# V and gate columns of all sixteen heads by Strassen, masks added by matmul, one projection unit per differential head

## The chip, the cores and the metric

The kernel runs on one core of a Trainium2 chip. The metric is device microseconds of one execution, the median of three runs. Five engines of the core appear in the profile: TensorE (PE, its weight loads PEld), VectorE (DVE), ScalarE (ACT), GpSimd (POOL) and SyncE (SP). DMAs are issued from the queues of SP, ACT and POOL and share 16 DMA engines.

## The reference, cut to what matters

One layer, 1024 tokens, width 2048. One projection feeds two groups of eight heads; each group has q, k, v and gate columns of width 1024.

```
hn = rmsnorm(x, norm_mix_g)                       # (1024, 2048)
proj = hn @ w_in                                  # (2048, 8192)
sb_q, sb_k, sb_v, sb_g, df_q, df_k, df_v, df_g = split(proj, -1)
# stick-breaking group: A[t,s] = beta_ts * prod_{s<j<t}(1-beta_tj), s < t
# differential group, partial rotary on 16 of 64 columns of each q and k half:
s  = q_c @ k_c.T * 64**-0.5,  c = 0, 1;   pr_c = softmax(where(mask, s, -inf))
df = (pr_0 - lam * pr_1) @ v;  df = rmsnorm(df, subln_g) * (1 - lambda_init)
mixed = concat([sb * silu(sb_g), df * silu(df_g)])
h = x + mixed @ w_out
h = h + sigmoid(rmsnorm(h, norm_ple_g) @ w_ple_gate) * (p @ w_ple_proj)
return rmsnorm(h, norm_final_g)
```

## The kernel before

All operands are float32. A product of two of them is made of three matmuls: each operand is split into a high part (a cast to fp32r, on ScalarE) and a low part (the difference, on VectorE), and high x high, high x low and low x high are accumulated in PSUM (L240 to L242, L634 to L636, L1750 to L1752). Activations lie transposed, features on partitions and 512 tokens (a *half*) as columns, with the token order reversed; the half with index 1 holds the first 512 tokens and is computed first.

The program has four stages.

1. *First stage* (to about 331 us). The V and gate columns of the eight stick-breaking heads, for both halves, by one level of Strassen's scheme: `Seven` (L585) runs seven products per unit in place of eight. A unit is one head; there are two phases, one for each half of the 2048 features, and a product is 12 matmuls of 128x512 (`product`, L629). Weights are loaded (`wload`, L672), combined by VectorE (`sources`, L683), split (`whigh`, `wlow`, L711 and L728), and results leave by `vput` (L839) to `vghalf_d` (phase 0), are read back as `hr` in phase 1, added, and written to `vg_d`. Sums of x for the next phase (`visit`, L977) and sums of squares of x (`squares`, L1031) are made alongside.
2. *Heads* (L1335 on): for each half, first the differential heads 8 to 15, then the stick-breaking heads 0 to 7. `unit` (L226) is 96 matmuls over four weight pieces of 128x1024 and gives 256 columns of the projection. A stick-breaking head has one unit (q, k) and reads V and gate from `vg_d`. A differential head has two: one for q and k, one for V and gate. Weight pieces are loaded by SP and split in `wprep` (L149; ScalarE L162, VectorE L157). After q and k are evicted (`taken`), the rotary steps and the splitting of q and k follow on VectorE and ScalarE.
3. *Output projection* by `Seven`, then 4. *the gate, the embedding and the last norm*.

Order: TensorE, VectorE and ScalarE run in the order in which the code emits instructions. Inside a head, `Side` (L199) holds a list of steps with a due time, counted in steps of three matmuls; `unit` ticks it after each group of three, so attention of one head (`attention`, L289: scores, `weights`, `values`, `turn`, `mix`, `norm`) is spread between the projection matmuls of the next heads. Due times are written out as numbers. Scores get their causal mask from VectorE, which adds a 128x128 tile in PSUM (`masked`, L320 to L326); in the fourth row block the differential score is one matmul of 256 columns (`side_by_side`, L312), since k's tile holds high and low parts side by side.

Two lines say what the rest hangs on, the units of the projection stream and the due times of a differential head:

```
units = [(ap["w_in"][hd][i], half, hd) for half, order in ((1, ORDER1), (0, ORDER0)) for hd in order for i in range(1 if hd < H else 2)]
s0, s1, s2, t0 = [0, 2], [5, 8], [12, 15], 19
```

## Time and profile before

| what | value |
|---|---|
| time, median of 3 | 2430.82 us (2429.68 to 2435.75) |
| profiled execution, its own time | 2428.5 us |
| its span | 2426.7 us |
| granted TensorE clock | 0.994 |
| DMA moved | 492.92 MB, mean 203 GB/s |
| chain that ended last | PE 84%, DVE 6%, DMA 4%, ACT 3% |

How to read the lines that follow in the prediction. A group's row gives line, engine, operation, tiles as out<-in, shapes and count; behind the first bar the busy time and the mean duration of one in ns; behind the second the idle time of that engine just before, and what ended it. A wait's row gives waiter, releaser, total us, times, longest. A window's row gives its length, then busy us (and count) of PE, PEld, DVE, ACT and POOL, the granted clock, the DMA engines' busy share and GB/s. A timeline row gives start and duration in us. Matmul durations are latencies that overlap, so their pace has to be read from starts.

### The profile page before, as it was taken

How to read it: one execution, taken by the hardware profiler on the slowest of the kernel's cores; microseconds unless marked ns; L12 is line 12 of the kernel's file. 1: busy time of each engine (PE TensorE's matmuls, PEld its weight loads, DVE VectorE, ACT ScalarE, POOL GpSimd, SP SyncE). 2: the span in 40 equal slices, each digit the busy share in tenths (PEclk: the TensorE clock that was granted, in tenths of full speed). 3: DMA queues.
4: the chain of work that ended last, by engine and by line, in shares of the span. 5: the costliest groups of instructions: out<-in, count | busy, mean ns of one | idle time of the engine just before them, and what ended most of it. 6: DMA issues, size and time to landing. Idle time of an engine off the chain costs nothing.

```text
span 2426.7 us, 32432 instructions
## 1 busy us (share of the span) xinstructions
PE 2364.6 (97%) x11262; PEld 1966.1 (81%) x11262; DVE 1862.1 (77%) x3233; ACT 1194.5 (49%) x2138; POOL 243.7 (10%) x368
## 2 busy tenths in 40 slices
PE   9999999999999999999999999999999998999997
PEld 7777878888888887888888888887778886878876
DVE  7887867777877777788888866667787877577788
ACT  6243335555556445555556566445534434532453
POOL 1211100000000000000000001011121221001000
PEclk9999999999999999999999999999999999999999
DMA  7876755444456777444444465667788999898965
GB/s 234 303 253 232 239 180 156 152 156 131 135 150 223 245 252 241 122 114 112 111 125 117 112 188 171 203 200 233 196 220 217 263 266 296 273 321 280 320 206 178
DMA packets 221604, 492.92 MB, mean 203 GB/s; under 512 B 24768, under 2 KB 37056, under 8 KB 221440
## 3 DMA queue, kind: packets, MB, share of 16 engines
q1 hardware_dynamic: 158224, 345.86, 43.6%
q0 software_dynamic: 43920, 109.86, 18.4%
q10 hardware_dynamic: 19296, 35.14, 4.2%
q8 instruction: 88, 1.44, 0.2%
q14 instruction: 76, 0.62, 0.1%
HBM read 336.09 MB, written 163.05 MB: 206 GB/s over the span
## 4 chain that ended last, share of the span: by engine, by line
PE 84%; DVE 6%; DMA 4%; ACT 3%; issue 2%; SPq 0%; ACTq 0%; POOL 0%; DVEq 0%; POOLq 0%
PE acc L242 14%; PE acc L240 14%; PE acc L241 14%; PE pbc L634 4%; PE pbc L635 4%; PE pbc L636 4%; PE tp L415 2%; PE z L319 1%; PE z L318 1%; PE pb L1750 1%; PE pb L1751 1%; PE pb L1752 1%; PE av L462 1%; PE av L461 1%; PE av L460 1%
## 5 line engine op out<-in xcount | busy, mean ns | idle before, releaser
L240 PE MATMUL acc<-xh,whi 128*128 128x512 f32 x1152 | 465.8, 404 | 0.0
L242 PE MATMUL acc<-xh,wlo 128*128 128x512 f32 x1152 | 452.1, 392 | 4.1 <-DVE wlo L157 4.1
L241 PE MATMUL acc<-xl,whi 128*128 128x512 f32 x1152 | 451.6, 392 | 0.0
L162 ACT CAST whi<-wraw 128x1024 fp32r<-128x1024 f32 x192 | 201.6, 1050 | 121.5 <-PE acc L241 113.9
L242 PEld LDWEIGHTS acc<-xh,wlo 128*128 128x128 f32 x1152 | 217.1, 188 | 53.4 <-DVE wlo L157 5.4
L725 ACT CAST wpr<-T 128x512 fp32r<-128x512 f32 x144 | 87.5, 620 | 341.9 <-DVE T L690 260.6
L241 PEld LDWEIGHTS acc<-xl,whi 128*128 128x128 f32 x1152 | 218.1, 189 | 37.7
L240 PEld LDWEIGHTS acc<-xh,whi 128*128 128x128 f32 x1152 | 217.4, 189 | 38.0
L157 DVE TENSOR_TENSOR wlo<-wraw,whi 128x1024 fp32r<-128x1024 f32 x160 | 195.1, 1220 | 49.4 <-ACT whi L162 48.0
L434 ACT CAST awh<-tp 128x256 fp32r<-128x256 f32 (+1 forms) x160 | 80.7, 504 | 162.2 <-PE tp L415 160.7
L370 ACT ACTIVATE et<-z,mx 128x512 f32<-128x512 f32 (+7 forms) x128 | 94.7, 740 | 61.7 <-DVE mx L364 53.3
L725 ACT CAST wpr<-wraw 128x512 fp32r<-128x512 f32 x112 | 68.5, 614 | 108.6 <-DMA wraw<-tw_d 38.6
L439 DVE TENSOR_TENSOR awl<-tp,awh 128x256 fp32r<-128x256 f32 (+1 forms) x160 | 92.3, 577 | 37.0 <-ACT awh L434 36.7
L349 DVE TENSOR_TENSOR_SCAN st<-pt 128x511 f32<-128x511 f32 (+3 forms) x64 | 86.7, 1355 | 24.2 <-ACT pt L342 22.7
L739 DVE TENSOR_TENSOR wpr<-wraw,wpr 128x512 fp32r<-128x512 f32 x112 | 76.0, 684 | 35.3 <-ACT wpr L725 35.1
L739 DVE TENSOR_TENSOR wpr<-T,wpr 128x512 fp32r<-128x512 f32 x144 | 98.6, 685 | 3.7 <-ACT wpr L725 1.1
L364 DVE TENSOR_REDUCE mx<-z 128x1 f32<-128x512 f32 (+7 forms) x128 | 97.0, 758 | 4.4
L634 PE MATMUL pbc<-cS,wpr 128*128 128x512 f32 x208 | 81.2, 390 | 1.4 <-DVE u L1111 1.1
L635 PE MATMUL pbc<-cS,wpr 128*128 128x512 f32 x208 | 80.9, 389 | 0.0
L636 PE MATMUL pbc<-cS,wpr 128*128 128x512 f32 x208 | 80.9, 389 | 0.0
L326 DVE TENSOR_TENSOR z<-z,masks 128x128 f32<-128x128 f32 x144 | 42.2, 293 | 45.9 <-PE z L316 31.5
L342 ACT ACTIVATE pt<-z 128x512 f32<-128x512 f32 (+3 forms) x64 | 41.6, 650 | 71.8 <-DVE z L326 69.9
(548 smaller groups left out, 6203.6 us busy)
## 6 DMA issues: line engine op xcount, KB each, us to landing
wraw<-w_in SPq DMA_DIRECT2D x192, 512.0 KB, 3.7
wraw<-w_gate SPq DMA_DIRECT2D x92, 256.0 KB, 5.8
wraw<-w_out SPq DMA_DIRECT2D x72, 256.0 KB, 4.5
wlo_d<-wlo SPq DMA_DIRECT2D x32, 512.0 KB, 3.0
wlo<-wlo_d SPq DMA_DIRECT2D x32, 512.0 KB, 3.4
wraw<-w_vg SPq DMA_DIRECT2D x58, 256.0 KB, 3.5
comb_d<-sg POOLq DMA_DIRECT2D x48, 256.0 KB, 7.4
h_d<-hc POOLq DMA_DIRECT2D x48, 256.0 KB, 4.8
```

Of the source, the lines that this page charges most:

```text
L157: V.tensor_tensor(lo[:, o], raw[:, o], hi[:, o].bitcast(F32), op=ALU.subtract)
L162: side.later(1, lambda: A.copy(hi[:, o], raw[:, o]))
L240: T.matmul(acc[c], hi[:, k2, kh, c, :], xh, start=first, stop=False)
L241: T.matmul(acc[c], hi[:, k2, kh, c, :], xl, start=False, stop=False)
L242: T.matmul(acc[c], lo[:, k2, kh, c, :], xh, start=False, stop=last)
L364: V.reduce_max(mx, z[:, vw], axis=AX.X, negate=True)
L370: A.activation(et[:, vw], z[:, vw], AF.Exp, bias=mx[:, 0:1], accum_out=l)
L634: T.matmul(o, wh[:, w], xh, start=start and k == 0, stop=False, skip_group_check=True)
L635: T.matmul(o, wh[:, w], xl, start=False, stop=False, skip_group_check=True)
L636: T.matmul(o, wl[:, w], xh, start=False, stop=k == 3, skip_group_check=True)
L725: A.copy(t[:, 0], src)
L739: V.tensor_tensor(t[:, 1], src, t[:, 0].bitcast(F32), op=ALU.subtract)
```

## The change

- The first stage makes V and gate of all sixteen heads: `Seven` with 16 units. The first product pair of heads 8 to 15 in phase 0 runs ahead as plain products (`opening`). Phase 1 no longer reads phase 0's results back: `vput` accumulates into `vg_d` in DRAM. The sums of squares of x move to phase 0.
- In phase 1, `weight_pieces` loads 30 pieces of the differential heads' q and k weights, splits them and stores high and low parts in `whi_d` and `wlo_d`. In the first half these pieces, and in the later half all pieces, are read from there (stick-breaking heads 3 to 7 of the later half read the raw weights and the low part).
- A differential head has one unit. The rotary columns of q and k are gathered into one tile `rot` by SBUF to SBUF DMAs, turned once for both, and copied back; the high parts go to q, qz and k by DMA too. V and gate come from `vg_d`.
- Masks of the differential scores are added by a bf16 matmul, identity x mask, between the two score matmuls; in the first half both softmaxes' scores share one PSUM tile (`pairs`). The fourth row block uses two matmuls of 256 columns.
- In the later stages operands of the gate are loaded in another order and the gate's products run A11 three times before A12; the last unit's S1 product comes after S3. Due times of all steps are new numbers.

The core of the diff:

```diff
-            units = [(ap["w_in"][hd][i], half, hd) for half, order in ((1, ORDER1), (0, ORDER0)) for hd in order for i in range(1 if hd < H else 2)]
+            units = [(ap["w_in"][hd][i], half, hd) for half, order in ((1, ORDER1), (0, ORDER0)) for hd in order for i in range(1)]
...
+    def is_made(pc, half, hd):
+        return half == 0 or hd >= H and 4 * (hd - H) + pc < PIECES
...
+        if made:
+            nc.sync.dma_start(hi.bitcast(F32), whi_d[hd, pc].bitcast(F32))
+            lastw[0] = nc.sync.dma_start(lo.bitcast(F32), wlo_d[hd, pc].bitcast(F32))
+            return hi, lo
...
-                elif side_by_side:
-                    T.matmul(o, q[:, c, rs], k[:, c, 3 * P:], start=True, stop=True)
...
                     T.matmul(o, q[:, c, rs], k[:, c, c0:HALF], start=True, stop=False)
+                    if ki == 0:
+                        T.matmul(z[:, rs], identb, masks[:, 1, :], start=False, stop=False, skip_group_check=True)
                     T.matmul(o, qz[:, c, rs], KL[:, ki, c0:], start=False, stop=True)
...
+        def pairs(rb):
+            z = pz.tile([P, 2, HALF], F32, name="z", tag="z")
...
-        gv = Seven(lambda u, ph, k: ap["w_vg"][u, ph, k], H, flow(H))
+        gv = Seven(lambda u, ph, k: ap["w_vg"][u, ph, k], 2 * H, flow(2 * H))
...
         def vput(o, ph, hf, blk, u):
-            G.dma_start((vg_d if ph else vghalf_d)[hf, blk, u], o)
+            G.dma_start(vg_d[hf, blk, u], o, **(dict(accum_op=ALU.add) if ph else {}))
...
+        def weight_pieces(u):
...
+                    nc.sync.dma_start(lo.bitcast(F32), ap["w_in"][hd][0][pc].rearrange("p a b c d -> p (a b c d)"))
+                def fn(hd=hd, pc=pc, lo=lo, hi=hi):
+                    A.copy(hi, lo.bitcast(F32))
+                    V.tensor_tensor(lo, lo.bitcast(F32), hi.bitcast(F32), op=ALU.subtract)
+                    for d, t in ((whi_d, hi), (wlo_d, lo)):
+                        G.dma_start(d[hd, pc].rearrange("p a b c d -> p (a b c d)").bitcast(F32), t.bitcast(F32))
...
-                if ph:
-                    V.tensor_tensor(u2, u2, r[1, 1], op=ALU.add)
...
-                if ph:
-                    gv.xq.extend((gv.slot + 3, fn) for fn in squares(u))
+                if ph and 2 * u < PIECES:
+                    weight_pieces(u)
+                if ph == 0 and 0 < u < 9:
+                    gv.xq.extend((gv.slot + 3, fn) for fn in squares(u - 1))
...
-        NEXT = {"A11": [("A11", 0)], "A12": [("A12", 0)], "S1": [("A11", 4)]}
+        NEXT = {"A11": [("A11", 0)], "S3": [("A11", 4, 3)], "S1": [("A11", 7, 1), ("A12", 0)]}
...
+                        for b in range(2):
+                            m = 64 * c + 32 * b
+                            nc.sync.dma_start(fs["r"].bitcast(F32)[m:m + 32, :], f[64 * b:64 * b + 32, :])
...
+                    def high(c, fs=fs, qk=qk):
+                        h = fs["sr"[c]]
+                        A.copy(h, fs[c].bitcast(F32))
+                        for b, r in enumerate(rows):
+                            for t, o in ((qk[0], r), (qk["qz"], r)) if c == 0 else ((qk[1], rows[0]), (qk[1], rows[1])):
+                                nc.sync.dma_start(t[o, b, 0:HALF].bitcast(F32), h[r].bitcast(F32))
...
-                    vacc = two_accs()
-                    unit(X, acc=vacc)
...
-GAPS, GAPD = 4, 6
+SC = ((20.5, 21, 23.5, 25.5, 29.5, 31.5, 34.0, 37.0), (24.5, 27, 34, 41))
+ROPE = ((3.5, 4.0, 6.0, 10.0, 11.6, 12.5, 15.0), (6.5, 7, 9.5, 12.5, 12.6, 13.5, 14))
```

Where instructions stand now. TensorE, the first scores of the first differential head of the half computed first; `z` is the score tile, `kl` and `qz` the low parts, `acc` the projection of the next unit. Before:

```order
L318 MATMUL z<-k,q 128x512
L319 MATMUL z<-kl,qz 128x512
L240 MATMUL acc_3248<-cA11h,whi 128x512
L241 MATMUL acc_3248<-cA11l,whi 128x512
L242 MATMUL acc_3248<-cA11h,wlo 128x512
```

Now:

```order
L427 MATMUL z<-k,q 128x512
L429 LDWEIGHTS identb
L429 MATMUL z<-masks,identb 128x128
L430 MATMUL z<-kl,qz 128x512
L427 MATMUL z<-k,q 128x512
L429 LDWEIGHTS identb
L429 MATMUL z<-masks,identb 128x128
L430 MATMUL z<-kl,qz 128x512
```

Both softmaxes' scores of a row block follow each other without projection matmuls between, each with a mask matmul and its own weight load in the middle.

SP's queue over one differential head of the half computed first; `wraw` is a raw weight piece, `mixed_d` and `comb_d` take a head's result. Before:

```order
L169 DMA wraw<-w_in 128x1024 x5
L1493 DMA h_d<-xT 128x512 x2
L169 DMA wraw<-w_in 128x1024 x3
L270 DMA mixed_d<-sg 128x512
L278 DMA comb_d<-neg 128x512 x3
```

Now (`rot` holds the rotary columns, `qk` the evicted q or k, `sw` and `rot` later also the high parts):

```order
L1612 DMA rot<-qk 32x512 x2
L183 DMA whi<-whi_d 128x1024
L184 DMA wlo<-wlo_d 128x1024
L1513 DMA vf<-vg_d 128x512
L1612 DMA rot<-qk 32x512 x2
L1513 DMA gf<-vg_d 128x512
L183 DMA whi<-whi_d 128x1024
L184 DMA wlo<-wlo_d 128x1024
L1629 DMA qk<-rot 32x512 x4
L291 DMA mixed_d<-sg 128x512
L299 DMA comb_d<-neg 128x512 x3
L1636 DMA q<-sw 64x512
```

The small copies stand between the weight loads on one queue, and each waits for VectorE or ScalarE.

POOL's queue in phase 1 of the first stage; `hc` is a result of a product, `wpiece` a weight piece. Before:

```order
L840 DMA vghalf_d<-hc 128x512 x13
L840 DMA vg_d<-hc 128x512 x25
L1339 DMA cs<-rope 128x2x512
L840 DMA vg_d<-hc 128x512 x7
L1428 MEMSET qz 128x1024 x2
```

Now:

```order
L950 DMA vg_d<-hc 128x512 x3
L1210 DMA whi_d<-wpiece 128x1024
L1210 DMA wlo_d<-wpiece 128x1024
L1210 DMA whi_d<-wpiece 128x1024
L950 DMA vg_d<-hc 128x512
L1210 DMA wlo_d<-wpiece 128x1024
L950 DMA vg_d<-hc 128x512 x3
```

Four stores of weight pieces, 512 KB each, stand among the four accumulating stores of a unit.

More of the change, by code (lines that the diff above doesn't have):

```diff
@@ L355, in three @@
                     ws[rb] = bt
-                side.later(1, one)
-                side.later(3, two)
-                side.later(5.5, three)
+                side.later(SBL[half][0], one)
+                side.later(SBL[half][1], two)
+                side.later(SBL[half][2], three)
                 return
@@ L475, in summed @@
                         mixed(half, hd, sg)
-            side.later(2, summed)
+            side.later(2 if sb else LM[half][1], summed)
             if sb:
@@ L493, in low @@
                 sqs[pr] = sq, sqh, sql
[L495 to L496 removed]
+            side.later(LM[half][2], squared)
+            side.later(LM[half][3], low)
         def norm(pr):
@@ L554, in attention @@
             if not sb:
-                steps.append((t + gap * n + (7 if tight else NORM_LAT), partial(norm, pr)))
+                steps.append((t + gap * n + NORM_LAT[half][pr], partial(norm, pr)))
         return steps
@@ new lines, in _body @@
+        gv.xq.extend((0, fn) for fn in todo)
+        for u in range(H, 2 * H, 2):
+            pair = []
+            for nm in ("A11", "A12"):
+                for j in range(2):
+                    if nm == "A11":
+                        pair.append(pp.tile([P, HALF], F32, name="pa", tag="acc", bufs=2))
+                    prod(u + j, 0, nm, pair[j], nm == "A11")
+                    o = ftile()
+                    A.copy(o, pair[j])
+                    if nm == "A11":
+                        G.dma_start(vgpart_d[u + j], o)
+                    else:
+                        vput(o, 0, 1, 0, u + j)
@@ L1085, in _body @@
         prev = None
         for ph in range(2):
[L1087 to L1095 removed]
+            for u in range(2 * H):
+                last = ph == 1 and u == 2 * H - 1
+                s1 = ev.tile([P, HALF], F32, name="s1", tag="sq", bufs=2)
```

596 lines of the change are left out of this document (365 added, 231 removed).

## The prediction

> **What bounds the kernel now.** I read the page first, its engine row and the summary of the chain that ended last:
>
> ```profile
> PE 2364.6 (97%) x11262; PEld 1966.1 (81%) x11262; DVE 1862.1 (77%) x3233; ACT 1194.5 (49%) x2138; POOL 243.7 (10%) x368
> PE 84%; DVE 6%; DMA 4%; ACT 3%; issue 2%; SPq 0%; ACTq 0%; POOL 0%; DVEq 0%; POOLq 0%
> ```
>
> PE holds 84% of the chain, so a matmul taken away is worth its pace and a wait of PE is worth its length. Next, busy time by stage: the differential heads of the half computed first, with 512 keys (331:740), and of the later half, with 1024 keys (960:1430); then the stretches from the output projection on. Columns: length, busy us of PE, PEld, DVE, ACT, POOL, clock, DMA share, GB/s.
>
> ```profile
> 331.00:740.00 409.00, 405.78 (x1914) 337.91 (x1913) 312.92 (x659) 219.82 (x432) 19.10 (x31) 1.00 0.47 144
> 960.00:1430.00 470.00, 467.82 (x2343) 395.34 (x2342) 383.89 (x698) 271.34 (x465) 32.18 (x45) 1.00 0.43 119
> 1690.00:1800.00 110.00, 103.62 (x510) 84.25 (x509) 85.21 (x137) 58.82 (x110) 18.64 (x22) 1.00 0.82 214
> 1800.00:1900.00 100.00, 99.50 (x440) 82.03 (x439) 80.48 (x128) 38.32 (x67) 19.44 (x25) 1.00 0.87 227
> 1900.00:2024.00 124.00, 122.77 (x539) 100.55 (x538) 99.33 (x153) 48.35 (x86) 35.69 (x51) 1.00 0.98 274
> 2024.00:2100.00 76.00, 67.91 (x280) 53.92 (x279) 46.66 (x74) 38.63 (x67) 5.66 (x8) 0.96 0.86 270
> 2100.00:2200.00 100.00, 94.59 (x408) 77.11 (x408) 70.33 (x115) 39.67 (x73) 10.78 (x15) 0.98 0.96 310
> ```
>
> The head stages leave PE almost no idle time and use less than half of the DMA engines; idle time sits in later stretches, where the DMA share is 0.82 to 0.98. The view of waits names PE's longest ones:
>
> ```profile
> PE pbc L634 <- DVE hc L1138: 5.0, 2, 2.6
> PE acc L242 <- DVE wlo L157: 4.6, 3, 2.2
> PE pa L1751 <- DVE cgA12l L619: 4.5, 1, 4.5
> ...
> PE pbc L634 <- DVE hc L1081: 3.5, 2, 2.7
> ```
>
> A busy matmul time is no price, since matmuls overlap. The timeline of PE gives the pace, start to start (first column; between the first two rows lie eleven more matmuls of 128x512):
>
> ```profile
> 902.04 0.39 PE L240 MATMUL acc<-cA12h,whi 128*128 128x512 f32 x1
> ...
> 904.80 0.28 PE L314 MATMUL z<-k,q 128*128 128x256 f32 x1
> 904.91 0.28 PE L315 MATMUL z<-k,q 128*128 128x256 f32 x1
> 905.03 0.28 PE L316 MATMUL z<-k,q 128*128 128x256 f32 x1
> 905.15 0.40 PE L240 MATMUL acc<-cA12h,whi 128*128 128x512 f32 x1
> ```
> ```profile
> 1693.91 0.60 PE L415 MATMUL tp<-ident,bt 128*128 128x128 f32 x4
> 1694.27 0.48 PE L634 MATMUL pa<-cA11h,wfhi 128*128 128x512 f32 x1
> ```
>
> So 2.76/12 = 0.230 us at 512 columns, 0.35/3 = 0.117 at 256, 0.36/4 = 0.09 for a 128x128 transpose; at 384 I take 0.17, between the first two.
>
> **The change part by part.**
>
> *Projection.* Sixteen second units (8 differential heads, 2 halves) of 96 matmuls go: 1536. Eight more Strassen units come: 8 x 2 phases x 7 products x 12 = 1344. Net 192 x 0.230 = 44.2 us less.
>
> *Scores.* In 32 score tiles (fourth row block) one matmul of 256 columns becomes two: 32 x 0.117 = 3.7 us more.
>
> *Masks.* 128 bf16 matmuls of 128x128 are new. No row shows bf16. From below, a quarter of a 512 matmul, 0.058; from above a whole one, 0.23, should the change of type or the extra weight load break the overlap; work added to a full PE excludes a gain. I take the nearest row, the transpose: 128 x 0.09 = 11.5 us (7.4 to 29.4). The masks that VectorE loses ended none of PE's long waits.
>
> *VectorE and ScalarE in the heads.* The unit that goes was cover: such a head had 470/8 = 58.8 us of PE and 48.0 of VectorE in the later half. By my count of matmuls it now has 116 of 512, 4 of 384, 52 of 256 and 38 of 128 columns: 26.7 + 0.7 + 6.1 + 3.4 = 36.9 us (29.0 in the first half, by 100, 4, 28 and 22). VectorE loses, by these groups,
>
> ```profile
> L157 DVE TENSOR_TENSOR wlo<-wraw,whi 128x1024 fp32r<-128x1024 f32 x160 | 195.1, 1220 | 49.4 <-ACT whi L162 48.0
> ...
> L326 DVE TENSOR_TENSOR z<-z,masks 128x128 f32<-128x128 f32 x144 | 42.2, 293 | 45.9 <-PE z L316 31.5 <-PE z L319 13.8
> ...
> L1458 DVE STREAM_SHUFFLE sw<-qk 128x512 f32<-128x512 f32 x32 | 23.5, 734 | 0.0
> ...
> L1450 DVE TENSOR_TENSOR q<-qk,q 64x512 fp32r<-64x512 f32 x32 | 22.0, 686 | 0.9
> ...
> L1454 DVE TENSOR_TENSOR k<-qk,k 64x128 fp32r<-64x128 f32 x64 | 18.1, 283 | 0.4
> ```
>
> 8 x 1.22 (weights now come split from DRAM), 10 masks at 0.29, one shuffle and three rotary products (0.73 + 3 x 0.69), and of 4 x 0.69 + 4 x 0.28 for q and k all but 2 x 0.69: 9.8 + 2.9 + 2.8 + 2.5 = 18.0. So 30.0 of 36.9, a share of 0.81 where it was 0.82; 39.1 - 18.0 = 21.1 of 29.0 in the first. I cost this at nothing: the share that hid it before hides it still. If that cover fails, the second rival is the price.
>
> *Waits that go.* The three waits on wlo L157 (4.6) fall with the subtraction: the first pieces of a half are fetched made. The gate operands are loaded in another order and A12's are first used one product later, which aims at the wait on cgA12l (4.5). 9.1 us less; either may come back as a wait on a DMA (0 to 9.1). The waits on hc (8.5) are PSUM banks that VectorE reads late; the four adds per unit of phase 1 that filled its queue there go, but units double. I leave them (plus or minus 8.5).
>
> *Steps that are moved.* The squares of x, 32 loads on ScalarE's queue with 30 adds of VectorE, and the sums of x move from phase 1 into phase 0 of the first stage, where a unit is 60 matmuls, 13.8 us of PE. VectorE has there 5 splits, 4 differences and 5 sums for the unit and 4 adds for the squares, 18 x 0.69 = 12.4 us: covered at 0.90. Uncovered, it shows in the waits on hc, whose bounds stand above. On SP the rotary copies each wait for VectorE or ScalarE, and the weight loads queued behind them wait along; those run up to two pieces ahead, 2 x 29.0/4 = 14.5 us, which hides them. Without that cover PE waits on whi, at up to a landing (3.7 to 5.8 us, rows below) a head.
>
> *DMA.* What pays for all this is traffic. The queues now:
>
> ```profile
> q1 hardware_dynamic: 158224, 345.86, 43.6%
> q0 software_dynamic: 43920, 109.86, 18.4%
> q10 hardware_dynamic: 19296, 35.14, 4.2%
> ```
>
> The changed program's own DMA rows sum to 424.4, 158.1 and 35.1 MB. At the present 3.06, 4.06 and 2.9 us a MB (share x 2426.7 / MB) that is 1299 + 642 + 102 = 2043 us, 85% of the span after 66%. Two stretches are tight. A phase 1 unit with a pair of weight pieces (15 of them) moves 5.25 MB in 84 x 0.230 = 19.3 us of PE, 272 GB/s. An early differential head moves 4.19 MB of weights, 1.84 of rotary copies, 1.31 of k and v, 0.52 of V and gate, 0.26 of x and 0.5 to 1.05 of results: 8.6 to 9.2 MB in 29.0 us, 297 to 317 GB/s. The row of 2100:2200 moved 310 at share 0.96, so 323 is there to be had, and 9.2 MB take 28.5 us: it fits, barely. Price of running that full: the row 1900:2024 (0.98) lost 1.2 of 124 us of PE, 1.0%; the row 2100:2200 lost 5.4%. Over 15 x 19.3 + 8 x 29.0 = 521 us: 5.2 us by the first, which is nearest in share, 0 to 28 as bounds.
>
> The Trainium skill (Perfetto Trace Analysis, Roofline) lets a core that runs alone draw about 435 GB/s through its 16 DMA engines. The trace disagrees: 0.98 busy at 274 GB/s, 0.96 at 310. By the page the 5.2 us would be nothing and the sum 5 us lower.
>
> *Sum.* The profiled execution took 2428.5 us for a span of 2426.7, and 2.3 less than the median of 2430.8. 2428.5 - 44.2 + 3.7 + 11.5 - 9.1 + 5.2 = 2395.6; beside the median, **2398 us**.
>
> **The rivals.**
>
> *DMA engines become the bound (slower).* Place: the two tight stretches. For it: accumulating stores and 288 small copies join them, and the row 1800:1900, with accumulating stores, gives only 227/0.87 = 261 GB/s. Against: 2100:2200. At 261 a head takes 33 to 35 us, 4 to 6 over its 29.0, 40 us for eight; a unit takes 20.1, 0.8 over, 12 for fifteen. 2398 - 5 + 52 = 2445. It turns the sign below some 265 GB/s.
>
> *The hops of the rotary copies become the chain (slower).* The issues by line, with median us to landing:
>
> ```profile
> wraw<-w_in SPq DMA_DIRECT2D x192, 512.0 KB, 3.7
> wraw<-w_gate SPq DMA_DIRECT2D x92, 256.0 KB, 5.8
> ...
> comb_d<-sg POOLq DMA_DIRECT2D x48, 256.0 KB, 7.4
> ...
> pw<-w_pp SPq DMA_DIRECT2D x32, 128.0 KB, 4.4
> ```
>
> Size hardly matters to landing, load does. Between k's eviction (step 31) and its first scores (32 + 24.5 in the first half, a step being 29.0/32 = 0.91 us) lie 23 us; in them now stand three copies in a row and some 6 us of VectorE and ScalarE. At 4.4 us a copy that is 19 and fits; at 7.4 it is 28, 5 us late in each of 16 heads: 80 us, 2478. It decides above 5.7 us a copy. The small copies also queue on SP behind weight loads that wait for a free buffer. The Trainium skill (DMA: Bandwidth & Descriptors, Bandwidth) speaks against them as well, calling transfers under 64 KB descriptor-dominated; those here are 64 and 128 KB, and the 128 KB row of this trace lands within 0.7 us of the 512 KB one.
>
> *VectorE and ScalarE hold PE up in the short heads (no change).* The stretch 1690:1800, where attention of the last head already shares PE with other products, idles 5.8%. Over 8 x 29.0 + 8 x 36.9 = 527 us that is 31: 2429. Against: equal VectorE share.
>
> *More waits go than I count (faster still).* If the hc waits (8.5) and half of the 13.5 us of idle PE in 2024:2200 beyond cgA12l (4.5) go too, and the DMA costs nothing: 2398 - 8.5 - 4.5 - 5.2 = 2380.
>
> That the change doesn't do what it says (fewer matmuls) is excluded by the count.
>
> **How the numbers follow.** Forecast 0.55; DMA bound 0.09; hops 0.05; short heads 0.11; more waits 0.20. The range must leave out the two slower rivals and little else: from 2380 with the masks at their floor (4 less) to the forecast with masks at their ceiling (18) and DMA halfway up (12): 2376 to 2428, taken to 2430 to hold the third rival. About 0.3%, 7 us, is what a measurement of this kernel tells from no change. Faster: forecast and more waits, 0.75. Same: 0.11. Slower: 0.14.
>
> **What would show it.** Right: about 8898 matmuls of 512 columns; mask matmuls at about 0.09 us of pace; PE's wait on wlo gone; the first stage ending near 640 us with DMA shares of 0.9 to 1.0 there and in the early heads, at 290 GB/s or more, and PE idle under 2%. Wrong: PE waits on whi or wlo from DRAM (first rival); on q, k or z, with copies landing after 6 us or more (second); on awl, lead or sm with VectorE over 0.9 (third).

## The result: slower by 1.4%, and the profile after

The changed kernel takes 2466.32 us (2460.97 to 2469.47, four runs) beside 2431.42 (also four) for the kernel before: ratio 1.0139, 95% interval 1.0115 to 1.0162. I had forecast 2398. Its profiled execution took 2461.0 us for a span of 2459.2; that of before took 2428.5.

The engine row and the summary of the chain, of the changed kernel's page:

```profile
PE 2358.3 (96%) x11230; PEld 1936.3 (79%) x11230; DVE 1754.9 (71%) x2954; ACT 1109.5 (45%) x2086; POOL 333.5 (14%) x496
...
PE 63%; DMA 16%; DVE 13%; ACT 4%; issue 3%; SPq 2%; DVEq 0%; ACTq 0%
```

VectorE and ScalarE have less to do than before, in number and in share of the span, and yet PE's part of the chain fell from 84% to 63% while that of DMAs rose from 4% to 16%. The matmuls went as counted; other things came to end last.

Where it came: the same cuts in both kernels, at the first projection matmul of each group of heads. Before (differential heads of the half computed first, its stick-breaking heads, then the same of the later half):

```profile
326.50:728.20 401.70, 398.48 (x1876) 331.27 (x1875) 305.95 (x640) 210.95 (x415) 20.68 (x33) 1.00 0.47 144
728.20:948.00 219.80, 219.18 (x1098) 184.28 (x1097) 166.50 (x306) 113.56 (x226) 12.68 (x19) 1.00 0.76 250
948.00:1409.80 461.80, 459.62 (x2297) 387.77 (x2296) 377.58 (x687) 263.70 (x454) 32.30 (x45) 1.00 0.43 119
1409.80:1653.50 243.70, 240.45 (x1285) 204.61 (x1284) 165.63 (x255) 130.04 (x209) 25.08 (x34) 1.00 0.62 188
```

After, the first stage in front and the same four groups:

```profile
0.00:623.10 623.10, 615.96 (x2698) 507.20 (x2699) 440.48 (x655) 249.83 (x409) 145.12 (x233) 1.00 0.87 270
623.10:869.90 246.80, 231.19 (x1131) 184.48 (x1129) 149.54 (x316) 103.57 (x267) 13.24 (x23) 0.99 0.89 276
869.90:1114.00 244.10, 230.40 (x1147) 190.97 (x1148) 180.84 (x333) 123.43 (x263) 14.87 (x24) 0.98 0.82 272
1114.00:1434.40 320.40, 297.44 (x1543) 239.10 (x1543) 219.74 (x426) 160.81 (x319) 28.00 (x39) 0.99 0.75 215
1434.40:1690.30 255.90, 250.56 (x1352) 212.25 (x1350) 179.35 (x282) 129.84 (x221) 29.14 (x38) 0.99 0.69 205
```

The first stage grew by 296.6 us (326.5 to 623.1), 12.5 less than the 309.1 of its 1344 matmuls at 0.230 us; 5.6 of them are the waits on hc, which fell from 8.5 to 2.9 us, and the rest is a pace a little under 0.230. The four groups of heads shrank by 259.8 us (1327.0 to 1067.2) where the terms of the sum that lie there (projection, scores, masks and the wait on wlo; 2.3 us for the DMA left aside) come to 342.7: **82.9 us are missing in the heads**. What follows them went from 773.2 to 768.9 us, as forecast. In the heads PE now idles 15.6, 13.7, 23.0 and 5.3 us where it idled 3.2, 0.6, 2.2 and 3.2, 48 us more; the other 35 are time in which PE counts as busy but its matmuls follow each other more slowly than I counted. VectorE's share there is 0.61 and 0.69 in the differential groups, not the 0.73 and 0.81 I had worked out.

The DMA engines are not the bound either. In the stretch of the first stage where they never rest, PE loses 0.8 of 298 us:

```profile
330.00:628.00 298.00, 297.21 (x1309) 245.23 (x1307) 194.72 (x281) 107.56 (x169) 90.51 (x126) 1.00 1.00 285
```

PE's longest waits name q, and what VectorE makes for the attention. (`awh` and `awl` are the high and low parts of the transposed attention weights, `lead` those of the first block, `sqv` a step of the head's norm, `et` and `l` exponentials and sums of the softmax, `vf` and `gf` a head's V and gate as loaded, `sg` its gate.)

```profile
PE tp L487 <- DVE sqv L608: 13.2, 13, 4.0
PE av L535 <- DVE awl L510: 10.9, 19, 2.1
PE z L427 <- DMA q<-qk: 10.8, 6, 5.1
PE z L338 <- DMA q<-qk: 8.6, 6, 6.7
PE av L530 <- DVE lead L509: 5.3, 3, 2.6
```

So one asks what VectorE, ScalarE and SP's queue wait for, in the differential heads of the later half (1114 to 1434.4; three answers):

```profile
DVE sw L1617 <- DMA rot<-qk: 16.6, 7, 6.8
...
DVE vf L1650 <- DMA vf<-vg_d: 8.5, 6, 2.4
```
```profile
ACT sg L1552 <- DVE gf L1650: 14.0, 7, 3.2
ACT sw L1633 <- DMA qk<-rot: 13.4, 4, 11.3
```
```profile
SPq L183 <- PE acc L264: 68.6, 18, 8.1
SPq L1629 <- DVE l L402: 49.7, 6, 9.1
SPq L1612 <- DVE l L404: 43.8, 7, 6.7
...
SPq L1636 <- DMA vf<-vg_d: 8.4, 5, 2.7
SPq L1636 <- DMA gf<-vg_d: 5.0, 6, 1.6
```

VectorE and ScalarE stop at steps whose operand is still in a copy. SP's queue, which also carries the weights and the loads of V and gate, stands at the rotary copies (L1612, L1629) until VectorE has got through the attention work that stands ahead of their operands. One head in SP's queue and then in the chain:

```profile
1278.60 2.41 SPq L1629 DMA_DIRECT2D qk<-rot  x4
1281.11 0.53 SPq L183 DMA_DIRECT2D whi<-whi_d  x1
1281.68 0.45 SPq L184 DMA_DIRECT2D wlo<-wlo_d  x1
1282.18 0.42 SPq L1513 DMA_DIRECT2D vf<-vg_d  x1
...
1285.73 5.34 SPq L1636 DMA_DIRECT2D k<-rot  x4
1291.17 1.19 SPq L1644 DMA_DIRECT2D q<-qk  x2
```
```profile
1268.29 4.92 DMA rot<-qk
...
1282.18 7.45 DMA vf<-vg_d
1289.66 0.69 DVE vf L1650
...
1290.68 0.68 DVE gf L1650
1291.38 0.64 ACT sg L1552
...
1293.37 0.69 DVE sg L1558
1294.06 0.61 DVE awl L510
1294.72 0.39 PE msq L576
```

V is issued only after the four copies back, takes 7.45 us to land, and VectorE, at its place in the order, stands at vf until 1289.66; behind it come gf, the gate on ScalarE and VectorE, and only then the awl for another head's attention, which is late for PE.

The rows on vf and gf in SP's list show one more wait, for DMAs whose data the waiting copy does not use: SP stands at a copy until the DMA that it issued eight places earlier has landed. In the head shown gf, two copies into q, two into qz and the four into k follow vf, so that the third and the fourth copy into k are the eighth after vf and after gf, and 3.2 of the 5.34 us of those four are these two waits. What sets the eight no run here shows.

### The profile page after: what moved, and what is told of

Same layout as the page of the kernel before. It is cut to its first block, busy times and chain, and to the rows that moved or that the text cites. A ratio compares the mean times of both kernels' runs of the same rounds, so it can differ in the third digit from the quotient of the medians.

```text
span 2459.2 us, 33022 instructions
## 1 busy us (share of the span) xinstructions
PE 2358.3 (96%) x11230; PEld 1936.3 (79%) x11230; DVE 1754.9 (71%) x2954; ACT 1109.5 (45%) x2086; POOL 333.5 (14%) x496
## 4 chain that ended last, share of the span: by engine, by line
PE 63%; DMA 16%; DVE 13%; ACT 4%; issue 3%; SPq 2%; DVEq 0%; ACTq 0%
PE pbc L726 6%; PE pbc L727 6%; PE pbc L728 6%; PE acc L262 5%; PE acc L264 5%; PE acc L263 5%; DMA rot<-qk 3%; PE pa L726 2%; PE pa L727 2%; PE pa L728 2%; PE tp L487 2%; DMA gf<-vg_d 2%; DMA q<-qk 1%; DMA wraw<-w_gate 1%; DMA wraw<-w_out 1%
## 5 line engine op out<-in xcount | busy, mean ns | idle before, releaser
L262 PE MATMUL acc<-xh,whi 128*128 128x512 f32 x768 | 314.2, 409 | 0.1
L264 PE MATMUL acc<-xh,wlo 128*128 128x512 f32 x768 | 303.0, 395 | 2.8 <-DVE wlo L195 2.5
L263 PE MATMUL acc<-xl,whi 128*128 128x512 f32 x768 | 301.5, 393 | 0.0
L264 PEld LDWEIGHTS acc<-xh,wlo 128*128 128x128 f32 x768 | 144.8, 189 | 37.1 <-DVE wlo L195 3.8
L263 PEld LDWEIGHTS acc<-xl,whi 128*128 128x128 f32 x768 | 145.7, 190 | 24.2
L262 PEld LDWEIGHTS acc<-xh,whi 128*128 128x128 f32 x768 | 145.7, 190 | 24.0 <-ACT whi L190 0.5
L831 DVE TENSOR_TENSOR wpr<-T,wpr 128x512 fp32r<-128x512 f32 x208 | 142.7, 686 | 11.3 <-ACT wpr L817 7.4
L950 POOL DMA_DIRECT2D vg_d<-hc x120 | 86.8, 724 | 331.1 <-DVE hc L1191 203.9
L726 PE MATMUL pbc<-cS,wpr 128*128 128x512 f32 x288 | 112.2, 389 | 0.8 <-DVE u L1247 0.8
L728 PE MATMUL pbc<-cS,wpr 128*128 128x512 f32 x288 | 112.0, 389 | 0.0
L727 PE MATMUL pbc<-cS,wpr 128*128 128x512 f32 x288 | 112.0, 389 | 0.0
L535 PE MATMUL av<-awl,v 128*128 128x256 f32 x256 | 74.9, 293 | 11.1 <-DVE awl L510 10.9
L533 PE MATMUL av<-awh,v 128*128 128x256 f32 x256 | 72.6, 284 | 1.3 <-ACT awh L505 1.2
```

What stands on the lines that cost most here:

```text
L262: T.matmul(acc[c], hi[:, k2, kh, c, :], xh, start=first, stop=False)
L263: T.matmul(acc[c], hi[:, k2, kh, c, :], xl, start=False, stop=False)
L264: T.matmul(acc[c], lo[:, k2, kh, c, :], xh, start=False, stop=last)
L726: T.matmul(o, wh[:, w], xh, start=start and k == 0, stop=False, skip_group_check=True)
L727: T.matmul(o, wh[:, w], xl, start=False, stop=False, skip_group_check=True)
L728: T.matmul(o, wl[:, w], xh, start=False, stop=k == 3, skip_group_check=True)
```

## The experiments

Theories: **A**, engines and scores wait for copies to land; **B**, a short head's own attention chain is too long, copies or not; **C**, the copies hold SP's queue. (The rival that DMA bandwidth binds is spoken against by the row at share 1.00; in the heads the share is 0.69 to 0.89.) Ratios are to the kernel before, run on the same chip, with 95% intervals. The medians of the kernel before lay between 2431.4 and 2434.4 us from set to set, so differences in us to the changed kernel's 2466 are good to some 3 us. "A head" below is from one head's first projection matmul to the next's, in the steady middle of a group: 31 to 32 us (first half) and 41 to 42 (later half) in the changed kernel, where I had forecast 29.0 and 36.9.

**1. Rotary copies left out.** In the changed kernel:

```diff
-                        for b in range(2):
-                            m = 64 * c + 32 * b
-                            nc.sync.dma_start(fs["r"].bitcast(F32)[m:m + 32, :], f[64 * b:64 * b + 32, :])
...
-                        r = fs["r"].bitcast(F32)
+                        r = fs[0].bitcast(F32)
...
-                                nc.sync.dma_start(fs[c].bitcast(F32)[64 * b:64 * b + 32, :], r[m:m + 32, :])
```

> The changed kernel without the eight rotary copies of a differential head: the four that gather rows into rot and the four that put them back are left out, and the turn is made in place on q's tile alone (so the rotary part of q and k is not the reference's). VectorE and ScalarE do exactly the same operations as in the changed kernel. The changed kernel is 2466 us; its differential heads run 31.9 and 41.5 us each where 29.0 and 36.9 were worked out, about 60 us in sixteen heads, and with their neighbours about 80 us of PE idle time. Theory A (VectorE and ScalarE, which run in order, stand behind the copies: sw waits for rot, qk waits for rot): half or more of that comes back, 2415 to 2435 us, and the waits of sw on rot (12.8 and 17.6 us in the two stretches) are gone from VectorE's list with PE's waits on awl and lead shrinking. Theory B (short heads lose because the chain from q and k to the scores has too little projection work beside it, whoever copies): 2455 to 2470 us. Theory C (SP's issues of 0.6 us each, eighteen in a head, hold the queue): eight of eighteen go, so less than half comes back, 2435 to 2455 us.

2427.32 us, 0.9976 (0.9964 to 0.9989). Eight copies of 64 KB cost 39 us; B has at most the rest.

**2. The ten other copies as engine work.**

```diff
-                                nc.sync.dma_start(t[o, b, 0:HALF].bitcast(F32), h[r].bitcast(F32))
+                                A.copy(t[o, b, 0:HALF], f[r])
```

> The changed kernel with the ten other copies of a differential head undone: ScalarE writes the high parts of q, qz and k straight into their tiles (eight casts of 64 partitions in place of two of 128), VectorE the low parts (four differences of 64 partitions in place of two of 128). The rotary copies stay. About 1.4 us more of VectorE and 3 to 4 us more of ScalarE in a head. Theory A (rotary copies hold the engines): little comes back, since the rot copies stay, 2450 to 2466 us, with PE's wait on q from qk (10.8 and 8.6 us) gone. Theory B: more engine work in a short head, 2466 to 2490 us. Theory C (SP's issues): ten of eighteen go, 2425 to 2445 us.

2461.83 us, 1.0116 (1.0098 to 1.0135). PE's waits on q from qk (10.8 and 8.6 us) went, and waits on awh (8.3) and et (10.6) came.

**3. Both together.** The edits of 1 and 2. (In 2 to 4 VectorE also writes the low parts of q and k straight into their tiles, in differences of 64 partitions.)

> Both of the former together: no copy inside the core is left in a differential head, eighteen fewer SP issues in each of sixteen heads; the turn is made on q's tile alone (its rotary part is not the reference's). VectorE has 1.4 us more in a head than the changed kernel. Theories A and C: the sixteen heads come down to the 29.0 and 36.9 us that their matmuls need, 2385 to 2410 us, PE idle below 2%. Theory B: still over 2440 us, with PE waiting on awl, lead and sm as before.

2432.35 us, 0.9992 (0.9982 to 1.0001): no better than the first. Neither side of the expectation was met. Run 10 will show that the extra casts and differences of ScalarE and VectorE have a price of their own.

**4. No copies, whole rotary step on VectorE.** As 3, with q and k each shuffled and turned as before the change:

```diff
+                        for c in range(2):
+                            fs["rs"[c]] = fs["r"] if c == 0 else ev.tile([P, HALF], F32R, name="sw", tag="f", bufs=4)
+                            V.stream_shuffle(fs["rs"[c]].bitcast(F32), fs[c].bitcast(F32), SWAP)
```

> As the former, but with the rotary part as before the change: both q and k are shuffled and turned whole, on VectorE, so nothing of the computation is left out. VectorE has 4.2 us more in each differential head than in the changed kernel, ScalarE 3 to 4 us. Theories A and C: the copies cost more than the VectorE work they save, 2400 to 2430 us, below both kernels. Theory B: VectorE goes from 0.69 to 0.8 of a head and the heads grow by about that work, 2490 to 2530 us.

2461.18 us, 1.0114 (1.0099 to 1.013). Four more operations of VectorE in each of 16 heads, 2.8 us a head by their durations, cost 29 us beside run 3: extra engine work in these heads shows.

**5. Masks alone, on the kernel before.**

```diff
+                    if ki == 0:
+                        T.matmul(z[:, rs], identb, masks[:, 1, :], start=False, stop=False, skip_group_check=True)
```

> One part of the change alone, on the kernel before: the 128 masks of the differential scores added by bf16 matmuls, and the fourth row block as two matmuls of 256 columns (k's tile loses the columns that held its low part there). Projection, rotary steps and loads are those of before. VectorE loses ten mask additions and four small differences in a head. By the price of the prediction (0.09 us a mask, 3.7 us for the fourth row blocks) 2431 + 15 = 2446 us. By the price read off the changed kernel's PE timeline (a score group with its mask is 0.12 us longer at 256 columns, 0.14 to 0.22 at 512) 2431 + 3.7 + 17 = 2452 us. If what VectorE is relieved of counts, 2431 us or below.

2457.56 us, 1.0098 (1.0082 to 1.0113): 23 us by the medians. In the profiled execution the groups of heads take 18.5 us more (1345.5 for 1327.0); another 10.6 lie outside them, where the edit changes nothing, so 18.5 is the better figure. I had 15.2. Relieving VectorE brought nothing. What a mask costs shows in the changed kernel's PE timeline (start, latency):

```profile
1257.83 0.33 PE L338 MATMUL z<-k,q 128*128 128x384 f32 x1
1258.00 0.23 PE L340 MATMUL z<-masks,identb 128*128 128x128 bf16 x1
1258.04 0.42 PE L341 MATMUL z<-kl,qz 128*128 128x384 f32 x1
1258.30 0.39 PE L338 MATMUL z<-k,q 128*128 128x512 f32 x1
```

The bf16 matmul itself takes 0.04 us of pace (1258.00 to 1258.04), but the matmul behind it takes 0.26 instead of 0.17. By the starts of all 128 masks in this trace the one behind takes 0.08 us more at 256, at 384 and at 512 columns: 0.12 us a mask, 15.4 us, and with 3.7 for the fourth row blocks 19.1.

**6. Masks back on VectorE, in the changed kernel.**

```diff
-MASKPE = True
+MASKPE = False
...
-                    if ki == 0:
-                        T.matmul(z[:, rs], identb, masks[:, 1, :], start=False, stop=False, skip_group_check=True)
...
-            if sb:
-                side.later(1, masked)
+            side.later(1, masked)
```

> The changed kernel with the masks of the differential scores back on VectorE, in PSUM, one tick after the score matmuls, in both halves; 128 bf16 matmuls go, all else stays. Saved on PE 17 us by the changed kernel's timeline (11.5 by the prediction); spent on VectorE 8 additions of 0.29 us or 4 of two tiles in a head, in the chain from scores to weights. Theory A (VectorE stands behind the copies and is late as it is): what PE saves is lost again by later awl and et, 2455 to 2470 us. Theory D (the masks on PE are the part that was mis-sized): 2445 to 2452 us.

2469.33 us, 1.0145 (1.013 to 1.016), the same as the changed kernel. What PE saves there it loses in waits (those on q came to 22.4 us after 19.4, on sqv to 18.5 after 13.2): as long as heads wait, the masks' price is hidden.

**7. Rotary copies on GpSimd's queue.**

```diff
-                                nc.sync.dma_start(fs[c].bitcast(F32)[64 * b:64 * b + 32, :], r[m:m + 32, :])
+                                G.dma_start(fs[c].bitcast(F32)[64 * b:64 * b + 32, :], r[m:m + 32, :])
```

> The changed kernel with the eight rotary copies of a head issued on GpSimd's queue instead of SP's; same copies, same engine work. Leaving those copies out gave 2427 us, so they cost 39 us. Theory A1 (what costs is the hop itself, issue to landing, with VectorE and ScalarE standing in order behind it): a GpSimd hop is no shorter, 2460 to 2490 us. Theory C (what costs is SP's serial issue of 0.6 us a copy, and weight, V and gate loads queued behind copies that wait for VectorE): 2430 to 2445 us.

2492.95 us, 1.023 (1.0202 to 1.0258). SP freed and still slower: against C as the whole cause, though not a clean test, since on GpSimd's queue the copies back into qk landed in 5.8 us by median in the later half, after 2.4.

**8. Rotary steps later.**

```diff
-ROPE = ((3.5, 4.0, 6.0, 10.0, 11.6, 12.5, 15.0), (6.5, 7, 9.5, 12.5, 12.6, 13.5, 14))
+ROPE = ((6.5, 7.0, 9.0, 14.0, 14.6, 16.5, 18.0), (10.0, 10.5, 13.0, 17.0, 17.6, 19.0, 20.0))
```

> The changed kernel with later due times of the seven rotary and splitting steps only: three ticks later in the later half (6.5 to 18 in place of 3.5 to 15), three and a half to six in the half computed first; scores, loads, copies and queues unchanged. Nothing is taken away. Theory A1 (VectorE and ScalarE reach the step before the copy has landed and hold up everything behind it): the waits of sw on rot and of qk on rot shrink from some 2 us a head each, 2435 to 2455 us, unless the scores then wait for q. Theory A2 (the chain of hops itself is too long for the time between k's eviction and its first scores): the scores come later by what the steps come later, 2470 to 2510 us, with PE's wait on q from qk above its 19 us.

2525.98 us, 1.0379 (1.0362 to 1.0396). The scores now wait for q:

```profile
PE z L427 <- DMA q<-qk: 50.3, 8, 7.2
```

**9. The attention later.**

```diff
-SC = ((20.5, 21, 23.5, 25.5, 29.5, 31.5, 34.0, 37.0), (24.5, 27, 34, 41))
-TT = ((32, 44, 30.0), (35.5, 52, 33))
+SC = ((24.5, 25, 27.5, 29.5, 33.5, 35.5, 38.0, 41.0), (28.5, 31, 38, 45))
+TT = ((36, 48, 34.0), (39.5, 56, 37))
```

> The changed kernel with the whole attention of a differential head four ticks later (SC and TT plus 4, both halves); rotary steps, copies, loads and queues unchanged. Nothing is taken away. Theory A2 (the chain of hops from k's eviction to the scores is longer than the time it is given; steps later cost 60 us): PE's waits on q from qk (10.8 and 8.6 us) go, and so do some of those on awl and sqv, 2440 to 2455 us. Theory A1 (VectorE and ScalarE stand in order behind the copies, whatever the scores do): 2460 to 2475 us. Theory B (the attention's own chain in a short head): no change, or a few us more at the seams between the stages, 2460 to 2475 us.

2539.05 us, 1.0426 (1.0406 to 1.0446), which no theory had. The wait on q went, as A2 said (10.8 and 8.6 us became 2.3), but PE's waits on sqv rose from 13.2 to 41.6 us, and ScalarE's timeline in one head shows what came:

```profile
1363.91 0.20 ACT L397 ACTIVATION_READ_ACCUMULATOR et<-z,mx 128x1 f32 x1
1370.91 0.62 ACT L1633 CAST sw<-qk 128x512 fp32r<-128x512 f32 x1 [6.80 <-DMA qk<-rot]
1372.13 0.62 ACT L1633 CAST rot<-qk 128x512 fp32r<-128x512 f32 x1 [0.59 <-DMA vf<-vg_d]
1372.65 0.58 ACT L505 CAST awh<-tp 128x512 fp32r<-128x512 f32 x1
```

ScalarE stands 6.80 us at the next head's copy, and awh, which PE needs for this head, stands behind it. With copies in the order, each shift of one list of steps against the other puts other work behind a copy.

**10. All eighteen copies left out, engine work unchanged.** As 1, and:

```diff
-                        h = fs["sr"[c]]
-                        A.copy(h, fs[c].bitcast(F32))
+                        A.copy(qk[c][:, 0, 0:HALF], fs[c].bitcast(F32))
...
-                T.matmul(o, q[:, c, rs], k[:, c, c0:HALF], start=True, stop=False)
+                T.matmul(o, q[:, 0, rs], k[:, 0, c0:HALF], start=True, stop=False)
```

> The changed kernel with all eighteen copies of a differential head left out, and no engine work in their place: ScalarE casts q and k whole into one plane of their tiles, the turn is made on q's tile, the scores of both softmaxes read that one plane (so the scores are not the reference's). VectorE, ScalarE and TensorE have the same number of operations of the same sizes as in the changed kernel. Leaving out only the rotary copies gave 2427 us. Theory A (the hops are all there is, and the difference of 2398 to 2466 us is theirs, but for some 5 us of masks): 2398 to 2410 us. Theory B (what is left after the rotary copies is the short heads' own chain): 2418 to 2428 us.

2404.2 us, 0.9875 (0.9861 to 0.989): **the copies cost 62 us**, and B is refuted at this load of the engines. The two differential groups:

```profile
628.00:852.40 224.40, 224.40 (x1132) 182.49 (x1131) 150.23 (x321) 104.05 (x270) 16.81 (x30) 1.00 0.75 251
...
1089.80:1378.60 288.80, 287.65 (x1543) 237.07 (x1542) 219.02 (x426) 160.92 (x318) 28.45 (x40) 1.00 0.62 192
```

PE has next to no idle time left (none and 1.2 us), with the same VectorE and ScalarE time as in the changed kernel; a head is 29.5 and 38.7 us. Run 3 took out the same copies at 1.4 us more of VectorE and 3 to 4 of ScalarE a head, and was 28 us slower than this.

**11. V and gate loaded earlier.**

```diff
-VGD = ((40, 47, 48, 49.0, 51.0), (37.5, 47.5, 47.5, 47.5, 55.5))
+VGD = ((31.5, 47, 48, 49.0, 51.0), (31.5, 47.5, 47.5, 47.5, 55.5))
```

> The changed kernel with the loads of V and gate of a differential head issued at tick 31.5 in place of 40 and 37.5; all else as it is. In the trace they are issued just ahead of the copies into q, qz and k and together with GpSimd's loads of the first half's k and v, and all of these land 7 to 8 us after their issue there. Theory A3 (a pile-up of transfers at that point makes the hops long): the copies into q land in 3 to 5 us, VectorE's wait on vf and ScalarE's on gf go, 2435 to 2455 us. Otherwise: 2460 to 2470 us.

2456.21 us, 1.0093 (1.0073 to 1.0113): 10 us of it.

**12. Longer heads.** One product of three accumulated twice:

```diff
+                    if pad:
+                        T.matmul(acc[c], hi[:, k2, kh, c, :], xl, start=False, stop=False)
```

> The changed kernel with 32 more matmuls of 128x512 in the projection of every differential head (each high by low product is accumulated twice, so q and k are not the reference's), 7.3 us of PE a head, 116 us in all; no step, copy or load moves. Theory A and B alike (PE waits in these heads for something that does not get longer with the projection): much of it is absorbed, by the 2.9 and 4.6 us a head that are lost now, 2510 to 2545 us. If PE is the bound in these heads after all, and its matmuls are slower than counted: 2466 + 116 = 2582 us.

2530.63 us, 1.0395 (1.0378 to 1.0412): 116 us of matmuls cost 64. A head is 36.8 and 45.2 us, about the 29.5 and 38.7 without copies plus 7.3. With 7.3 us more cover the copies are hidden in these heads.

**13. The copies read by nobody.** Kernel 10 with eighteen copies of the same sizes back on SP, at the same places, into tiles that no engine reads (VectorE still waits before it overwrites what a copy reads: 11.9 and 6.2 us at the start of the two halves, at most 2.2 in any other head):

```diff
+                        for b, r in enumerate(rows):
+                            for o in (qk["qz"][r, 0, :], qk["qz"][r, 1, :]) if c == 0 else (fs["r"][r], qk[1][r, 1, 0:HALF]):
+                                nc.sync.dma_start(o.bitcast(F32), h[r].bitcast(F32))
```

> The kernel with all copies left out (2404 us), and eighteen copies of the same sizes put back on SP's queue at the same places of the code, behind the same steps; they write tiles that no engine reads, so nothing waits for them to land (the scores are again not the reference's). Theory A (VectorE, ScalarE and the scores wait for the landings): 2400 to 2412 us. Theory C (SP's time to issue, the queue behind it, and the traffic): 2435 to 2465 us.

2438.54 us, 1.0025 (1.0012 to 1.0039): in C's range, and about half way between 2404 and 2466. So some 28 of the 62 us are waits for landings (A), and 34 are not. The steady heads of the half computed first are 29.5 us, as without copies, at a DMA share of 0.94: there issue and traffic cost nothing. Those of the later half are 40 to 42 (one 38.7).

**14. The same, V and gate at tick 26**, ahead of the copies.

```diff
-VGD = ((40, 47, 48, 49.0, 51.0), (37.5, 47.5, 47.5, 47.5, 55.5))
+VGD = ((26, 47, 48, 49.0, 51.0), (26, 47.5, 47.5, 47.5, 55.5))
```

> The kernel with the eighteen copies issued and moved but read by nobody (2438 us; scores not the reference's), with one edit: V and gate of a head are loaded at tick 26, ahead of its first copies on SP's queue. If the 34 us that were left are V and gate held up on SP behind copies that wait for VectorE: the heads of the later half go from 40 to 42 us to 38.7, 2410 to 2422 us. If they are traffic, or SP's time to issue for the weights: 2432 to 2442 us.

2425.86 us, 0.9969 (0.9953 to 0.9985): 13 of the 34 are V and gate held up in SP's queue (C). Most of the rest lies at the seam of the half computed first, where the raw weights of the first stick-breaking heads queue behind the last copies. ScalarE's wait for them there, in this kernel (0 in kernel 10):

```profile
ACT whi L190 <- DMA wraw<-w_in: 15.9, 2, 8.0
```

The heads at that seam are 34.6, 38.2 and 36.1 us, and 29.5, 30.7 and 34.8 without copies: 13.9 us. What is left, some 8 us, no run assigns. In this kernel's profile it lies in the later half (its second head takes 34.4 us for 29.6 without copies, three others 39.5 to 40.7 for 38.7), where VectorE still waits 13.8 us for copies to finish before it overwrites what they read, and PE 3.6 us for wlo.

**15. The ten copies out, the rotary ones in.** Of the edits of 10 only those shown there.

> The changed kernel without the ten copies into q, qz and k (casts into one plane, which both softmaxes' scores read, so the scores are not the reference's); the eight rotary copies stay, and the engine work is that of the changed kernel. Leaving out the rotary ones alone gave 39 us, all of them 62. If the two parts add up: 2466 - 23 = 2443 us. If the second part only shows where the first is gone (the chain is as late as its rotary hops make it): 2455 to 2466 us. If either alone is enough to bring the chain in time: 2425 to 2435 us.

2422.88 us, 0.9962 (0.9949 to 0.9975): 43 us. With 39 for the others that is more than 62 for both; either set gone brings most of the chain in time. It also means that the shares of 28, 13 and 14 us hold for the order in which things were taken away here; another order would share the 62 us out otherwise.

**16. to 18. Ways to keep the gain.** Low part of q written directly, V and gate at 31.5:

```diff
-                            V.tensor_tensor(fs[0], f, h, op=ALU.subtract)
                             for b, r in enumerate(rows):
-                                nc.sync.dma_start(qk[0][rows[1 - b], b, :].bitcast(F32), f[r])
+                                V.tensor_tensor(qk[0][rows[1 - b], b, :], f[r], h[r], op=ALU.subtract)
```

> The changed kernel with V and gate loaded at tick 31.5 (2456 us alone) and the low part of q written by VectorE straight into its tile, two differences of 64 partitions in place of one of 128 and two copies: one hop less in front of the scores for 0.69 us of VectorE a head. Theory A: the waits of PE on q from qk (9.2 and 7.2 us with early V and gate) go, 2436 to 2448 us. If VectorE's extra time costs as much: 2452 to 2462 us.

2444.42 us, 1.0059 (1.0039 to 1.0079). GpSimd's arithmetic in place of all copies:

```diff
+                                G.tensor_tensor(sw, sw, cs[:, 1, :], op=ALU.mult)
+                                G.tensor_tensor(f, f, cs[:, 0, :], op=ALU.mult)
```

> The changed kernel without any copy between partitions and with nothing of the computation left out: q and k are shuffled whole by VectorE, the rotary products and sums and half of the high parts are made by GpSimd, which is idle in these heads, V and gate are loaded at tick 31.5. VectorE has as many operations as in the changed kernel, ScalarE two more casts a head. If GpSimd keeps up (ten operations a head in 29 us): 2404 to 2420 us, below both kernels. If an operation of GpSimd on 128x512 takes 2 us or more, or slows VectorE, the chain is late again: 2450 us and above.

2467.42 us, 1.0154 (1.0133 to 1.0175). An operation there takes twice VectorE's 0.69 us:

```profile
L1621 POOL TENSOR_TENSOR qk<-qk,cs 128x512 f32<-128x512 f32 x32 | 47.3, 1477 | 0.0
```

Casts on ScalarE and GpSimd in place of ten copies, V and gate at 26:

```diff
+                            A.copy(qk[c][r, b, 0:HALF], f[r])
+                            G.tensor_copy(qk["qz"][r, b, 0:HALF] if c == 0 else qk[1][rows[1 - b], b, 0:HALF], f[r])
```

> The changed kernel with nothing of the computation left out: V and gate loaded at tick 26; the ten copies into q, qz and k replaced by casts, four of 64 partitions on ScalarE and four on GpSimd (0.73 to 0.79 us each in the run with its arithmetic), and the low parts written straight by VectorE, 1.4 us more a head; the rotary copies stay. The same copies left out without engine work gave 2423 us. If GpSimd's casts stay off the chain: 2423 + 11 for VectorE - 10 for V and gate, 2418 to 2432 us, at or below the kernel before. If ScalarE's and VectorE's extra operations make attention late as they did with all eight casts on ScalarE (2462 us): 2445 to 2460 us.

2440.24 us, 1.0028 (1.0018 to 1.0038), the best that computes everything: 26 us below the changed kernel, not below the one before.

## Why the prediction was wrong

- **The step that failed** is the price of nothing for the small copies: "the weight loads queued behind them wait along; those run up to two pieces ahead, [...] which hides them", with the second rival's arithmetic ("at 4.4 us a copy that is 19 and fits"), by which copies cost nothing below 5.7 us. Their medians were 2.2 to 4.9 us, and they cost 62. In the later half those into q and qz took 7.1, beyond the 6 us that I had named as a sign of this rival, but three in a row (3.9 + 2.4 + 5.0 for k or 7.1 for q) came to 11.3 to 13.4 us there, still under 3 x 5.7.
- **What the runs showed in its place.** I had added up one chain from k's eviction to the scores. But a copy is a place in several queues at once. On VectorE or ScalarE the attention of another head stands behind the step that reads it (28 us, with the scores' own waits; the sum had no term for this). On SP the copy stands until VectorE comes to it, and V, gate and the weights stand behind the copy (13 us for V and gate, some 14 at the seam, 8 open). For the weights of the steady heads of the half computed first the cover held: 29.5 us with unread copies as without. Two pieces ahead there are only for those made weights; the raw pieces at the seam, and the later half, have one (`take`), and V and gate are due only 10 ticks (half computed first) and 7 (later half) ahead of the step that reads them.
- **The second rival** came near in time (2478 for 2466), and that is luck: its 80 us were for copies of 7.4 us and scores that wait 5 us in each of 16 heads, while PE waited for q 19.4 us in all. Its condition was too hard to meet. The Trainium skill (DMA: Bandwidth & Descriptors, Bandwidth), cited there, calls transfers under 64 KB descriptor-dominated; the copies here, at 64 and 128 KB, are not under it, and the trace shows no price of size: the 64 KB copies landed in 2.2 and 4.7 us by median, the 512 KB pieces of made weights in 4.1 and 5.2.
- **"The share that hid it before hides it still"** held only just. With the copies gone, PE is full (224.40 of 224.40 us) with unchanged engine work; but runs 3 and 4 show that nothing is to spare: 2.8 us of VectorE more a head cost 1.8.
- **Matmuls**: right (8906 of 512 columns, for about 8898). Without copies the time is 2404, and the sum said 2398. In that kernel's groups of heads (1004.2 us) 19.9 us are still missing: 3.3 are masks, 3.8 are idle time of PE (13.1 us for 9.3 before), and the rest is pace that no run explains.
- **Masks**: 15.2 us with the fourth row blocks, measured 18.5 in the heads. The nearest row was the wrong one: a mask's own pace is 0.04 us, not 0.09, but the matmul behind it loses 0.08.
- **Waits that go**: wlo fell from 4.6 to 2.5, cgA12l from 4.5 to 0.3, hc from 8.5 to 2.9 us, more than the 9.1 that I had taken off.
- **DMA near its limit**: the 5.2 us did not show; share 1.00 at 285 GB/s cost PE 0.8 of 298 us. The price by the Trainium skill (Perfetto Trace Analysis, Roofline), nothing, was nearer, though the engines were busy all the time far below the 435 GB/s or so that it names.

## What to carry to other kernels

Price a small copy between partitions by what stands behind it in every queue it touches, not by its landing time along one chain: the queue that issues it and the engine that reads it both stop there. In this case taking PE work out of a stage took away the cover of all that is hidden in it; so ask how long each hidden chain is before a stage is shortened, and try it with a kernel that leaves the suspect out and one that keeps it but lets nobody read it. Here shifting either list of steps made things worse (runs 8 and 9), and removing entries from an engine's order was worth more than moving them.

## What was not expected of the hardware

A bf16 matmul of 128x128 among fp32 ones costs 0.04 us itself and about 0.08 more in the one behind it (0.26 for 0.17 at 384 columns). DMA engines at a busy share of 1.00 (285 GB/s) left PE 99.7% busy. Issuing a copy from SBUF to SBUF took SP 0.5 to 0.6 us each, eighteen of them about 11 us of a 30 us head. SP held a DMA back until the one issued eight places earlier had landed: in the changed kernel 16 us at the copies into q, qz and k (9.3 on vf, 5.8 on gf, 0.9 on wlo).
